# Layer 0's mixture of experts: token rows by indirect DMA and transposes instead of one-hot products, and the overflow block in line as a 33rd expert

## The chip, the core and the metric

The kernel runs on one core of one Trainium2 chip. The metric is the device time of one execution in microseconds. The engines are TensorE (PE in the profile; its weight loads are PEld), VectorE (DVE), ScalarE (ACT), GpSimd (POOL) and SyncE (SP). All weights come from HBM through DMAs that SP issues; POOL issues a few DMAs of its own. Each engine works through its own queue in order.

## The reference

A trunk of two layers over 256 latent tokens (`x`) and 256 context tokens (`ctx`) of width 1024. Each layer is a mixer (layer 0: neighbourhood attention and a state-space branch; layer 1: two kinds of attention), a layer norm, and a mixture of 32 experts with two experts per token, chosen within one of four groups. Layer 0 sends all 512 tokens through its experts, layer 1 only the 256 latent ones. What the change touches:

```python
def hier_moe(h, wg, bg, we, be, w1, w3, w2):
    ...
    gate = g_gate * jax.nn.softmax(e_top, axis=-1)
    expert = g_sel * MOE_EXPERTS_PER_GROUP + e_idx
    return grouped_expert_mlp(h, expert, gate, w1, w3, w2)

def expert_block(args):          # inside grouped_expert_mlp
    xi, e = args                 # the rows of the tokens that chose expert e
    return (jax.nn.silu(xi @ w1[e]) * (xi @ w3[e])) @ w2[e]
...
out = jnp.zeros((t_tok + 1, dm), h.dtype).at[slot_tok].add(yb * slot_w[:, None])
```

An expert's weights are two matrices of 1024x512 and one of 512x1024, 6.29 MB in float32.

## The kernel before

`moe` handles one layer's experts. Every expert has 64 slots (`CAP`); `dest` holds for each token its two slot numbers, and tokens that find no slot among the 64 go to overflow blocks of 64 slots (`odest`), of which the first is nearly always used and further ones run in a loop on a count found at run time. Tokens lie in tiles of 128: four in layer 0 (`nt == 4`), two in layer 1.

Experts are gathered in groups of four (256 slots). `onehots` writes a 0/1 matrix of tokens by slots, and `gather` multiplies the token rows with it, so that the result is the group's rows, transposed, in `xg`. The rows are kept as a high and a low part (`h2h`, `h2l`), and a gather has four steps (`jp`), each of 4 tiles x 2 parts x 2 = 16 products of 128x256 into the PSUM tile `pg`. `gather_ahead` does the first three tiles of group 0 before the last tile is there. `group_gates` gets the gate of each slot by a product of the one-hot matrix with `gdr` (`pgs`, then `gs`), in two halves of 128 slots.

The loop in `moe` is a software pipeline over the experts. In turn e it issues the first half of the up-projection of expert e (`expert_up`, PSUM tile `a`), two combine steps, a gather step, the transposes of the expert before (`hp`), the second half of the up-projection, two more combine steps, and the down-projection of the expert before (`py`). A combine step (`combine_steps`) multiplies a pair of experts' outputs (`yh`, `yl`) with the turned one-hot matrix (`poT`, `ohT`) into `pcm`; VectorE multiplies it with a row of the modulation (`ym`), and POOL or VectorE adds it to the residual `S`. `pg` and `pcm` share a pair of PSUM buffers. Matrix products are kept in program order (`mmp`, `trp`); what else runs is ordered by a scheduler.

Weights go through a ring of twelve 1 MB buffers, eight called `ringw` and four called `raw` (`whalf`), so loads run up to two experts ahead. SP issues them in order, each when its buffer is free.

After the loop comes `overflow`: if there is a first block, `block` loads one expert's weights by a number read from `ov`, and computes it, start to end, on rows that were gathered during the last experts (`block_first`); then further blocks follow in a second loop. Behind it the layer norm scales the four tiles of `S`, and `mixer1` begins with transposes of `S` (`xT`) and products with weights that `unit` loads and splits (`w1h`, `w1l`).

Of the kernel before, what the change touches and what calls it, by code (L numbers as in the profile page):

```python
# [27 lines left out]
I32 = mybir.dt.int32  # L28
# [39 lines left out]
class Trunk:  # L68
# [68 lines left out]
    def run(self):  # L137
# [9 lines left out]
        self.mods = self.dram.tile([2, 2, 6144], F32, name="mods")  # L147
        self.prow = self.dram.tile([2, 2, 2, DM], F32, name="prow")
# [30 lines left out]
    def late_consts(self):  # L179
        nc, I = self.nc, self.I  # L180
        nc.gpsimd.dma_start(self.iota, self.bcast(I['iota'], 256))
        nc.gpsimd.dma_start(self.istack, I['istack'])
        nc.gpsimd.memset(self.one2, 1.0)
# [219 lines left out]
    def moe_tiles(self, nt):  # L403
        mp = self.moep
        self.h2h = mp.tile([128, nt, 8, 128], F32R, name="h2h")
        self.h2l = mp.tile([128, nt, 8, 128], F32R, name="h2l")
# [447 lines left out]
    def enter_moe(self, pool, layer, i, t, rows, R, nt):  # L854
# [126 lines left out]
    def moe(self, layer, tiles):  # L981
# [4 lines left out]
        with ExitStack() as es:  # L986
            with self.pool("exp", "right") as ep:
# [9 lines left out]
                def group(q):  # L997
                    ohs[q] = self.onehots(ep, nt, self.dest, 256.0 * q, 256) if q else self.oh0
                    X[q], st = self.gather(ep, nt, ohs[q], 256, None if q else self.pg0)
                    steps.extend(st)  # L1000

                def gates(q):
                    gs[q] = self.group_gates(ep, nt, ohs[q], 4 * q)
# [25 lines left out]


                for e in range(33):
                    cur = cur if e == 0 else begin(e) if e < 32 else None
                    if e % 2 == 0 and e < 32:
# [4 lines left out]
                    fill(2 if e > 28 else 1, steps)  # L1038
# [7 lines left out]
                    if e % 4 == 2 and e < 28:  # L1046
# [4 lines left out]
                    if prev:  # L1051
                        k = (e - 1) % 2
                        c = C[(e - 1) // 2]
                        if k == 0:
                            self.combine_turn(ep, nt, c)
                        self.expert_down(prev, c, k)
                        if k:
                            todo += self.combine_steps(ep, tiles, c)
                    if e == 0:
                        group(1)  # L1060
                        fill(2, steps)
# [33 lines left out]
    def group_gates(self, ep, nt, oh, e):  # L1095

        gs = ep.tile([64, 4], F32, name="gs", bufs=2)
        for i in range(2):
            pg = self.ps([128, 2, 32], "pgs")
            for t in range(nt):  # L1100
                self.mmp(pg.rearrange("p a b -> p (a b)"), oh[:, t, 128 * i:128 * i + 128], self.gdr[:, t], start=(t == 0), stop=(t == nt - 1))
# [758 lines left out]
```

## Time and profile before

| | us |
|---|---|
| median of 3 runs | 1883.29 |
| lowest and highest | 1879.22, 1886.46 |
| profiled execution | 1881.46 |
| its span, first to last instruction | 1879.6 |

| busy in the span | us | share |
|---|---|---|
| TensorE (products) | 1721.9 | 92% |
| VectorE | 975.9 | 52% |
| ScalarE | 507.7 | 27% |
| GpSimd | 358.3 | 19% |

Layer 0's experts take roughly 570 to 1130 us of the span, the first overflow block up to 1158, and layer 1's experts the last 480 us. Products are pipelined: a product's duration in a row is longer than the distance to the next one, so the distance between two starts is what a series of products costs. A row of the order of time shows the start, the time to the end of the last of the merged instructions, the engine, the line and operation, what it writes and reads, how many instructions were merged, and in brackets how long the engine stood idle before and what released it.

### The profile page before, as it was taken

What the parts mean: (1) busy time and instruction counts of PE and PEld (TensorE: products, weight loads), DVE (VectorE), ACT (ScalarE), POOL (GpSimd) and SP (SyncE); (2) the same over time, 40 slices, a digit from 0 to 9 for tenths busy, and PEclk for the clock granted to TensorE, in tenths of its full rate; (3) what the DMA queues carried; (4) which work ended last, traced back from release to release, by engine and by line L of the source; (5) the groups of instructions that cost most, each with busy time, mean ns of one, the idle gap of its engine ahead of it and who ended that gap; (6) DMA issues with size and microseconds to landing.
All of it is one profiled execution on the core that took longest, in us unless ns stands there. A gap on an engine that the chain in (4) does not pass through costs nothing. (4 is left out here: it accounts for less than half of the span.)

```text
span 1879.6 us, 22554 instructions
## 1 busy us (share of the span) xinstructions
PE 1721.9 (92%) x8481; PEld 915.1 (49%) x8481; DVE 975.9 (52%) x2007; ACT 507.7 (27%) x986; POOL 358.3 (19%) x297
## 2 busy tenths in 40 slices
PE   6999989988999999999999984889979999999995
PEld 3665656666555444444444441766444444444442
DVE  2454579896664453444443455774463433333335
ACT  2423344443212111111111111457431112111111
POOL 2212124443104111111111112422030100100101
PEclk9999999999999999999999986889989999999997
DMA  9655366645437999999999941345249999999993
GB/s 330 222 188 180 102 207 206 219 153 160 188 124 302 419 370 362 368 372 368 380 359 361 378 176 58 106 150 191 112 164 419 420 419 419 419 420 420 419 420 154
DMA packets 100371, 526.52 MB, mean 280 GB/s; under 512 B 20320, under 2 KB 24416, under 8 KB 46624
## 3 DMA queue, kind: packets, MB, share of 16 engines
q1 hardware_dynamic: 97456, 517.59, 71.5%
q0 software_dynamic: 2800, 7.42, 1.2%
q8 instruction: 70, 1.15, 0.2%
q14 instruction: 45, 0.37, 0.1%
HBM read 523.76 MB, written 1.20 MB: 279 GB/s over the span
## 5 line engine op out<-in xcount | busy, mean ns | idle before, releaser
L193 PE MATMUL a<-ringw,xg 128*64 128x512 f32 x1584 | 366.0, 601 | 0.8 <-DVE xg L1642 0.8
L193 PEld LDWEIGHTS a<-ringw,xg 128*64 128x64 f32 x1584 | 112.5, 138 | 208.7 <-issue 197.2
L1123 DVE TENSOR_TENSOR ym<-pcm,mod 128x512 f32<-128x512 f32 x136 | 90.6, 687 | 186.5 <-PE pcm L193 185.5
L1694 DVE TENSOR_TENSOR yl<-py,yh 64x512 fp32r<-64x512 f32 x130 | 89.4, 688 | 184.0 <-ACT yh L1693 183.9
L1124 POOL TENSOR_TENSOR S<-S,ym 128x512 f32<-128x512 f32 x68 | 87.1, 1281 | 466.8 <-DVE ym L1123 466.8
L1693 ACT ACTIVATE yh<-py 64x512 fp32r<-64x512 f32 x130 | 76.8, 591 | 297.3 <-PE py L193 247.8
L193 PE MATMUL py<-ringw,g 128*64 128x512 f32 x640 | 151.9, 617 | 0.5 <-ACT g L1677 0.5
L1124 POOL TENSOR_TENSOR S<-S,two 128x512 f32<-128x512 f32 x32 | 40.9, 1277 | 411.6 <-DVE two L1123 411.6
L193 PE MATMUL a<-raw,xg 128*64 128x512 f32 x496 | 116.0, 606 | 1.8 <-DMA raw<-in_moe_w_dram 1.8
L105 PE MATMUL pfm<-hTh,wh 128*128 128x512 f32 x256 | 105.8, 415 | 8.2 <-ACT up L639 5.5
L193 PE MATMUL pg<-two,h2h 128*128 128x256 f32 x408 | 90.6, 304 | 18.4 <-DVE ym L1123 10.4
L212 PE MATMUL adaps<-adw,cs 128*32 128x512 f32 x384 | 96.6, 645 | 11.5 <-DMA adw<-in_ada_w_dram 11.4
L100 POOL TENSOR_TENSOR wl<-raw,wh 128x512 fp32r<-128x512 f32 (+1 forms) x46 | 59.8, 1306 | 231.1 <-ACT wh L99 173.9
L106 PE MATMUL pfm<-hTh,wl 128*128 128x512 f32 x256 | 103.1, 403 | 0.0
L107 PE MATMUL pfm<-hTl,wh 128*128 128x512 f32 x256 | 101.0, 401 | 0.0
L1668 ACT ACTIVATE sa<-a 64x512 f32<-64x512 f32 x65 | 38.4, 591 | 222.3 <-PE a L193 222.3
L193 PE MATMUL pcm<-yh,ohT 128*128 128x512 f32 (+1 forms) x200 | 91.9, 460 | 6.8 <-DVE ym L1123 4.0
L1123 DVE TENSOR_TENSOR two<-pcm,S 128x512 f32<-128x512 f32 x64 | 42.7, 688 | 95.6 <-PE pcm L193 95.1
L193 PE MATMUL py<-raw,g 128*64 128x512 f32 x400 | 91.4, 598 | 0.5 <-ACT g L1677 0.5
L193 PEld LDWEIGHTS pg<-two,h2h 128*128 128x128 f32 x408 | 64.8, 196 | 49.3 <-DVE ym L1123 21.7
L193 PE MATMUL pg<-two,h2l 128*128 128x256 f32 x408 | 84.0, 288 | 2.0 <-DVE h2l L49 2.0
L193 PEld LDWEIGHTS py<-ringw,g 128*64 128x64 f32 x640 | 45.0, 141 | 83.6 <-issue 77.9
(510 smaller groups left out, 2931.9 us busy)
## 6 DMA issues: line engine op xcount, KB each, us to landing
ringw<-in_moe_w_dram SPq DMA_DIRECT2D x278, 1024.0 KB, 10.3
raw<-in_moe_w_dram SPq DMA_DIRECT2D x112, 1024.0 KB, 8.3
adw<-in_ada_w_dram SPq DMA_DIRECT2D x96, 512.0 KB, 5.4
raw<-in_w_in_dram SPq DMA_DIRECT2D x18, 1024.0 KB, 7.2
bc<-atd SPq DMA_DIRECT2D x16, 512.0 KB, 6.7
raw<-in_w_out_dram SPq DMA_DIRECT2D x4, 1024.0 KB, 5.1
raw<-in_o_w_out_dram SPq DMA_DIRECT2D x4, 1024.0 KB, 5.1
bias<-in_rpb_dram SPq DMA_DIRECT2D x8, 256.0 KB, 4.5
```

The costliest lines, as they stand in the source:

```text
L100: (eng or nc.vector).tensor_tensor(lo, src, hi, OP.subtract)
L105: mm(out, ah, bh, start=start, stop=False)
L106: mm(out, al, bh, start=False, stop=False)
L107: mm(out, ah, bl, start=False, stop=stop)
L193: return self.tc.keep_in_program_order(self.nc.tensor.matmul(*args, **kw))
L212: self.nc.tensor.matmul(p[32 * g:32 * g + 32, :], self.cs[:, j, :], w[:, (g - g0) * 512:(g - g0 + 1) * 512], start=(j == 0), stop=(j == 7))
L1123: nc.vector.tensor_tensor(m, p, self.rows5[t // 2][:, k], OP.mult)
L1124: (nc.gpsimd if i % 2 == 0 else nc.vector).tensor_tensor(S[:, t, k], S[:, t, k], m, OP.add)
L1668: self.nc.scalar.activation(s, a[0:64, :], AF.Silu)
L1693: nc.scalar.activation(c[h][0][r], py[q], AF.Copy)
L1694: V.tensor_tensor(c[h][1][r], py[q], c[h][0][r], OP.subtract)
```

## The change

In layer 0, each token tile's `h2` is stored by SP to an array in HBM, `h2d`. The number of each token stands as a 33rd column beside the gates in `gdr`, so that the product that yields the gates of a slot yields the number of its token too. VectorE copies that number to an integer tile `ix`, and POOL issues an indirect DMA that brings the 128 rows of 4 KB of half a group into `rows`, a tile that takes the memory of `h2l`. `turn_rows` transposes them into `pg`: a step is four transposes instead of 16 products. Group 0 and all of layer 1 gather as before. The gates of a group are made ahead of its rows, in the first expert of the group before; two turn steps stand in the second expert, one each in the third and fourth.

The first overflow block becomes expert 32 of the loop, always computed, with its weights' place read by SP; its one-hot matrix is made in expert 28's turn, its rows are fetched and its gates computed in expert 29's, and its steps stand in those of 30 and 31. Only further blocks are left behind the loop. Ahead of those SP issues the first loads of layer 1 (`ahead1`), and two tiles of `S` are scaled by VectorE and two by ScalarE, not three and one.

```diff
@@ enter_moe
+        if nt == 4:
+            nc.sync.dma_start(self.h2d[128 * i:128 * i + 128, :], h2)
@@ moe
+                    if q == 0 or nt == 2:
+                        X[q], st = self.gather(ep, nt, ohs[q], 256, None if q else self.pg0)
+                        steps.extend(st)
+                    else:
+                        if q == 1:
+                            self.rows_begin()
+                        rows = self.next_rows()
+                        X[q], st = self.turn_rows(ep, rows, 256)
+                        steps.extend([lambda: gates(q, rows)] + st)
...
                 def begin(e):
+                    if e == 32:
+                        at = nc.values_load(self.ov[0:1, 0:1], engines=[mybir.EngineType.SP], min_val=0, max_val=31)
+                        return self.expert_begin(ep, layer, None, B['xg'][:, :, 0, :], lambda: B['gs'], load=self.expert_at(layer, at))
...
+                nb = 33 if nt == 4 else 32
+                for e in range(nb + 1):
+                    cur = cur if e == 0 else begin(e) if e < nb else None
+                    if e == 32 and cur:
+                        C[16] = B['c']
...
-                    fill(2 if e > 28 else 1, steps)
+                    fill(2 if e > 28 or nt == 4 and e % 4 == 1 else 1, steps)
...
-                    if e % 4 == 2 and e < 28:
+                    if e % 4 == 2 and e < 28 and nt == 2:
                         gates(e // 4 + 1)
...
+                if layer == 0:
+                    self.ahead1 = {n: self.unit_raw(n, 256) for n in ('o_gkv', 'o_gq0')}
+                    self.rings, self.ring_k = self.rings[:1], 0
                 self.overflow(ep, layer, tiles, B)
...
-                    if t != 2:
+                    if t % 2 == 0:
                         V.tensor_scalar(S[:, t], S[:, t], r, m, op0=OP.mult, op1=OP.add)
@@ new functions
+    def fetch(self, ep, row, p):
+        n = p.shape[0]
+        ix = ep.tile([128, 1], I32, name="ix", bufs=4)[:n]
+        self.nc.vector.tensor_copy(ix, p)
+        self.nc.gpsimd.indirect_dma_start(row, None, self.h2d[:, :], bass.IndirectOffsetOnAxis(ap=ix, axis=0))
...
+    def turn_rows(self, ep, rows, n):
...
+        def step(jp):
+            p = self.ps([128, 2, 256], "pg")
+            for i in range(2):
+                for a in range(0, n, 128):
+                    m = min(128, n - a)
+                    self.trp(p[:, i, a:a + m], rows[:m, a // 128, 2 * jp + i::8])
...
@@ group_gates
+            if rows is not None:
+                self.fetch(ep, rows[:, i], pg[:, 0, 32:33])
@@ route_rest
+        self.gdr = self.ep.tile([128, nt, 2, 33], F32R, name="gdr")
...
+        V.tensor_copy(self.gdr[:, :, 0, 32], self.tok[:, 0:nt])
+        V.tensor_copy(self.gdr[:, :, 1, 32], self.tok[:, 0:nt])
@@ block_first
+            if nt == 4:
+                B['oh'] = self.onehots(ep, nt, self.odest, float(NSLOT), CAP)
+                return
...
+        def rows():
+            B['xg'], B['steps'] = self.turn_rows(ep, self.block_rows(ep, nt, B['oh']), CAP)
...
+        return B, [begin, rows, rest] + turn if nt == 4 else [begin] + turn + [rest]
@@ overflow
+        if nt == 4:
+            return more()
```

How the queues change at the places that the prediction speaks of. On TensorE, part of a turn of the loop in the middle of a group before (`a` are up-projections, `py` down-projections):

```order
L193 MATMUL a_5009<-ringw,xg 64x512 x8
L193 MATMUL pcm<-yh,ohT 128x512
L193 MATMUL pcm<-yl,ohT 128x512
L193 MATMUL pcm<-yh,ohT 128x512
L193 MATMUL pcm<-yl,ohT 128x512
L193 MATMUL pg<-two_4794,h2h 128x256 x2
L193 MATMUL pg<-two_4794,h2l 128x256 x2
```

and at the same place after:

```order
L197 MATMUL a_5056<-ringw,xg 64x512 x8
L197 MATMUL pcm<-yh,ohT 128x512
L197 MATMUL pcm<-yl,ohT 128x512
L197 MATMUL pcm<-yh,ohT 128x512
L197 MATMUL pcm<-yl,ohT 128x512
L201 MATMUL pg<-ident,rows 128x128 x4
L201 MATMUL hp<-ident,sa 128x64 x4
```

The pair of `h2h` and `h2l` rows stands four times in a row before; four transposes take the place of those eight rows.

On POOL, at the start of the expert stage, before:

```order
L1022 DMA yh<-in_ln_g_dram 128x512
L1022 DMA yl<-in_ln_b_dram 128x512
L1025 TENSOR_TENSOR S<-S,yh 128x512 x6
L1025 TENSOR_TENSOR S<-S,yl 128x512
L1025 TENSOR_TENSOR S<-S,yh 128x512 x2
L1025 TENSOR_TENSOR S<-S,yl 128x512 x7
```

and after:

```order
L1043 TENSOR_TENSOR S<-S,yh 128x512 x4
L1126 DMA rows<-h2d,ix 128x1024
L1043 TENSOR_TENSOR S<-S,yh 128x512 x2
L1043 TENSOR_TENSOR S<-S,yl 128x512
L1043 TENSOR_TENSOR S<-S,yh 128x512 x2
L1126 DMA rows<-h2d,ix 128x1024
L1043 TENSOR_TENSOR S<-S,yl 128x512 x7
```

The two fetches of the first group's rows stand among the sixteen operations that scale and shift `S`, behind the fourth and the ninth.

On VectorE, at the entry of layer 1, after (the statistics, the two splits, the reciprocal root, of which the first rows stand here, and the scaled tiles):

```order
L841 BN_STATS lnst<-S 128x6 x8
L842 BN_AGGR lnmv<-lnst 128x2 x2
L100 TENSOR_TENSOR w1l<-raw,w1h 128x512
L842 BN_AGGR lnmv<-lnst 128x2
L100 TENSOR_TENSOR w1l<-raw,w1h 128x512
L842 BN_AGGR lnmv<-lnst 128x2
L844 TENSOR_SCALAR lnn<-lnmv 128x4
```

Before, the four BN_AGGR stand together, the two splits come behind the root, one of them ahead of the three tiles of `S` and one behind them; now the splits are among the statistics and two tiles of `S` follow the root.

## Rows read from the trace of the kernel before

**Rows 1.** The page, busy time: engine, us, share of the span, instructions.

```profile
PE 1721.9 (92%) x8481; PEld 915.1 (49%) x8481; DVE 975.9 (52%) x2007; ACT 507.7 (27%) x986; POOL 358.3 (19%) x297
```

**Rows 2.** Stretches: length; PE, PEld, DVE, ACT, POOL busy (instructions); clock, DMA share, GB/s.

```profile
611.00:658.00 47.00, 45.72 (x222) 20.61 (x222) 22.13 (x39) 7.88 (x15) 6.42 (x5) 1.00 1.01 418
...
768.00:836.00 68.00, 64.26 (x322) 30.58 (x320) 31.25 (x52) 11.01 (x20) 10.26 (x8) 1.00 0.95 370
...
1400.00:1800.00 400.00, 390.51 (x1863) 164.86 (x1860) 143.49 (x241) 76.92 (x144) 43.08 (x34) 1.00 1.01 418
```

**Rows 3.** TensorE's waits, 577 to 1092 us: us in total, times, longest.

```profile
PE pgs L193 <- DVE gs L1103: 12.5, 8, 1.9
```

**Rows 4.** Order of time, TensorE, in layer 0's experts.

```profile
615.65 3.60 PE L193 MATMUL a<-ringw,xg 128*64 128x512 f32 x16
...
804.88 0.50 PE L193 MATMUL pg<-two,h2h 128*128 128x256 f32 x2 [0.39 <-DVE ym L1123]
...
806.98 0.69 PE L197 MATMUL hp<-ident,sa 64*128 64x64 f32 x4
807.60 3.65 PE L193 MATMUL a<-ringw,xg 128*64 128x512 f32 x16
...
1091.64 3.60 PE L193 MATMUL a<-ringw,xg 128*64 128x512 f32 x16
```

**Rows 5.** Order of time, TensorE, at the entry of layer 1.

```profile
1185.27 0.62 PE L189 MATMUL xT<-ident,S 128*128 128x128 f32 x4
1185.65 0.48 PE L321 MATMUL pgk<-w1h,h1Tl 128*128 128x256 f32 x2
```

**Rows 6.** SP's order of time, then two POOL transfers: KB each, us to landing.

```profile
547.59 2.04 SPq L426 DMA_DIRECT2D raw<-in_moe_w_dram  x2
551.02 2.04 SPq L426 DMA_DIRECT2D ringw<-in_moe_w_dram  x2
...
mod<-mods POOLq DMA_DIRECT2D x1, 512.0 KB, 8.9
...
mod<-mods POOLq DMA_DIRECT2D x1, 512.0 KB, 3.9
```

**Rows 7.** Order of time at the start of the expert stage, TensorE and POOL.

```profile
586.68 3.65 PE L193 MATMUL a<-ringw,xg 128*64 128x512 f32 x16
...
600.65 3.60 PE L193 MATMUL a<-ringw,xg 128*64 128x512 f32 x16
...
583.79 7.50 POOL L1025 TENSOR_TENSOR S<-S,yh 128x512 f32<-128x512 f32 x6 [11.94 <-ACT yh L1023]
```

**Rows 8.** Order of time around the last experts and the block.

```profile
1096.30 0.39 PE L193 MATMUL pgs<-one,ovg 128*64 128x2 f32 x4
...
1101.02 1.06 PE L197 MATMUL poT<-ident,two 128*64 128x128 f32 x4 [0.24 <-DVE ovgs L1711]
...
1111.26 0.69 DVE L1124 TENSOR_TENSOR S<-S,ym 128x512 f32<-128x512 f32 x1
...
1130.47 7.09 PE L193 MATMUL a<-ringw,xg 128*64 128x512 f32 x32
...
1146.29 0.50 PE L193 MATMUL pcm<-yh,ohT 64*128 64x512 f32 x1 [0.69 <-ACT yh L1693]
...
1156.17 1.26 POOL L1124 TENSOR_TENSOR S<-S,ym 128x512 f32<-128x512 f32 x1 [1.23 <-DVE ym L1123]
...
1156.72 1.25 DVE L1124 TENSOR_TENSOR S<-S,ym 128x512 f32<-128x512 f32 x1
```

**Rows 9.** Order of time at the entry of layer 1, VectorE and TensorE.

```profile
1160.81 4.84 DVE L837 BATCH_NORM_STATS2 lnst<-S 128x6 f32<-128x512 f32 x8 [2.83 <-issue]
...
1172.91 1.77 DVE L100 TENSOR_TENSOR w1l<-raw,w1h 128x512 fp32r<-128x512 f32 x1 [4.49 <-ACT w1h L99]
...
1174.61 5.10 DVE L1076 TENSOR_SCALAR S<-S,rsq_y,lnm 128x1024 f32<-128x1024 f32 x3
...
1183.11 0.56 PE L319 MATMUL pgk<-w1h,h1Th 128*128 128x256 f32 x1
```

More of the change, by code (lines that the diff above doesn't have):

```diff
@@ L147, in run @@
         self.mods = self.dram.tile([2, 2, 6144], F32, name="mods")
+        self.h2d = self.dram.tile([512, DM], F32, name="h2d")
         self.prow = self.dram.tile([2, 2, 2, DM], F32, name="prow")
@@ L1028, in moe @@
                 prev = None
-                for e in range(33):
-                    cur = cur if e == 0 else begin(e) if e < 32 else None
-                    if e % 2 == 0 and e < 32:
+                nb = 33 if nt == 4 else 32
[3 more added lines that the diff above has]
+                        C[16] = B['c']
+                    elif e % 2 == 0 and e < 32:
                         C[e // 2] = dict(oh=ohs[e // 4], sl=slice(64 * (e % 4), 64 * (e % 4) + 128))
@@ new lines, in next_rows @@
+    def next_rows(self):
+        self.rows_n = 1 - self.rows_n
+        return self.rows[:, self.rows_n]
+    def turn_rows(self, ep, rows, n):
+        nc, V = self.nc, self.nc.vector
+        k = n // 64
+        xg = ep.tile([128, 8, 4, 64], F32, name="xg", bufs=2)
+        def step(jp):
[4 more added lines that the diff above has]
+                    self.trp(p[:, i, a:a + m], rows[:m, a // 128, 2 * jp + i::8])
+            o = xg[:, 2 * jp:2 * jp + 2, 0:k, :]
+            src = p[:, :, :n].rearrange("p i (e s) -> p i e s", s=64)
+            if jp % 2:
+                nc.scalar.activation(o, src, AF.Copy)
+            else:
+                V.tensor_copy(o, src)
+        return xg, [lambda jp=jp: step(jp) for jp in range(4)]
@@ L1098, in group_gates, with block_rows @@
+    def block_rows(self, ep, nt, oh):
+        p = self.ps([CAP, 2], "pgs")
+        for t in range(nt):
+            self.mmp(p, oh[:, t, :CAP], self.gdr[:, t, 0, 31:33], start=(t == 0), stop=(t == nt - 1))
+        rows = self.next_rows()
+        self.fetch(ep, rows[:CAP, 0], p[:, 1:2])
+        return rows
+    def group_gates(self, ep, nt, oh, e, rows=None):
+        gs = ep.tile([64, 4], F32, name="gs", bufs=3)
         for i in range(2):
-            pg = self.ps([128, 2, 32], "pgs")
+            pg = self.ps([128, 2, 33], "pgs")
@@ L1126, in combine_steps, with unit_raw @@
         return [lambda i=i, t=t, h=h: step(i, t, h) for h in range(2) for i, t in enumerate(tiles)]
+    def unit_raw(self, name, w):
+        return [self.load([128, 4, w], self.I[name][:, 4 * i:4 * i + 4]) for i in range(2)]
     def mixer1(self):
@@ L1204, in unit @@
             def unit(name, w, eng=V):
-                raws = [self.load([128, 4, w], I[name][:, 4 * i:4 * i + 4]) for i in range(2)]
+                raws = self.ahead1.pop(name, None) or self.unit_raw(name, w)
                 hi = pp.tile([128, 8, w], F32R, name="w1h", bufs=2)
@@ L1725, in rest, with expert_at @@
             self.combine_turn(ep, nt, B['c'], CAP)
-        return B, [begin] + [lambda j=j: B['steps'][j]() for j in range(4)] + [rest]
+        turn = [lambda j=j: B['steps'][j]() for j in range(4)]
+        return B, [begin, rows, rest] + turn if nt == 4 else [begin] + turn + [rest]
+    def expert_at(self, layer, e):
+        return lambda nm: self.I[nm][layer, ds(e, 1)].rearrange("a b c -> (a b) c")
     def block(self, ep, layer, tiles, e, xg, c):
-        load = lambda nm: self.I[nm][layer, ds(e, 1)].rearrange("a b c -> (a b) c")
-        E = self.expert_begin(ep, layer, None, xg, c['gs'], load=load)
+        E = self.expert_begin(ep, layer, None, xg, c['gs'], load=self.expert_at(layer, e))
         for k in range(2):
@@ L1752, in more @@
                 oh = self.onehots(ep, nt, self.odest, base, CAP)
-                xg, steps = self.gather(ep, nt, oh, CAP)
+                xg, steps = self.turn_rows(ep, self.block_rows(ep, nt, oh), CAP) if nt == 4 else self.gather(ep, nt, oh, CAP)
                 for step in steps:
```

34 lines of the change are left out of this document (16 added, 18 removed).

## The prediction, written before the changed kernel ran

> **What bounds the kernel now.** I read the page first: TensorE is busy 92% of the span [rows 1]. A share of the whole span says nothing on one stage, so the table by stretches came next [rows 2]. The change lives in layer 0's experts, about 577 to 1130 us. There TensorE is busy 64.3 of 68 us while the loads run at 370 GB/s; in the expert stage of layer 1 (1400 to 1800 us) they run at 418 GB/s, and so they did for a while at the start of layer 0's stage. So 418 is what the loads can do, and in layer 0 they have some 12% in hand: TensorE sets the pace there, not the weights. The third view, TensorE's order of time, shows the period: the first up-projection of expert 3 starts at 615.65, that of expert 31 at 1091.64 [rows 4]: 476.0 us for 28 experts, 17.0 each, 68.0 a group of four. What TensorE waits for in that stretch is little: the second half of the gate products waits for VectorE, 12.5 us in 8 times [rows 3], and the one-hot gather waits 0.39 us for a PSUM buffer [rows 4]. Shortening TensorE's own work in the loop therefore shortens the stage, until the loads end last.
>
> **The loop.** A gather step (16 products of 128x256) runs from 804.88 to 806.98, where the transposes of hp start: 2.10 us [rows 4]. The new step is four 128x128 transposes of a tile read with stride 8. The trace of before has that very form at the entry of layer 1: four issued at 1185.27, the next instruction at 1185.65 [rows 5], 0.38 us, and with 0.1 us to the next 0.48. Each step saves 1.62 us. Between those two up-projections lie 28 steps (six groups and the block), so 45.4 us. Against it: in every fourth expert two turns now stand together, and the second takes the PSUM buffer that the last combine product has only just filled. It waits for one more VectorE product, about the 0.39 us of the gather's wait plus one 0.69 us operation [rows 4, 8], 1.1 us, seven times: 7.5 us. The block's gates, which stood behind expert 31's first up-projection, move to expert 29 and so into this stretch: from 1096.30 to 1101.02, 4.7 us [rows 8]. The gates of a group move from the third expert to the first of the group ahead, and cost what they cost now (the same wait for VectorE). Their 66th column and two small index copies are taken at nothing, under the wait of [rows 3]; without it they are some 0.3 us a group. Sum: 476.0 - 45.4 + 7.5 + 4.7 = 442.8 us.
>
> Does the other limit allow it? 28 experts read 28 x 6.29 MB = 176.1 MB; the rows add 6 x 1.05 MB and the block's 0.26, together 182.7 MB, which at 418 GB/s [rows 2] is 437 us. That is 6 us under TensorE's 442.8: the two limits now nearly meet, where before they were 12% apart. Two queues that are both almost full do not run at the larger of the two, so I allow 3 us: **gain 30**. The ends: 36 (loads at the best rate, second turns free), and 15 (each row read costs twice its bytes, 453 us, and another 1 us in each of eight fetches).
>
> **The start of the stage.** Here the change adds a wait. Expert 1 wants the first two turns right after its first up-projection, and their rows must have been fetched. In POOL's queue, the second piece of order above, the first fetch stands behind four of the multiplications of S, the second behind five more. That train starts at 583.79 and each takes 1.25 us [rows 7], so the first fetch is issued at 588.8. How long POOL needs for an indirect fetch no row shows; I take the length of its neighbour, 1.25 us, where a plain one takes less. The second is then issued at 588.8 + 1.25 + 6.25 + 1.25 = 597.6. Landing: a POOL transfer of the same 512 KB took 3.9 us with the queues empty and 8.9 us when at least four loads of 1 MB had been issued in the 6.2 us before it [rows 6]; in the middle, 604. TensorE is ready for the turns at about 589 (up-projection of expert 1 now from 586.68 [rows 7], about a microsecond earlier without the products before it). So it stands still for about 15 us. Then the two turns, hp, the second up-projection, poT and the down-projection take about 9.3 us, and expert 2 begins at 613.3 instead of 600.65 [rows 7]. Expert 2 itself is 3.3 us shorter (no gather step, no gates). **Loss about 10**, ends 4 and 18. Behind the fetches nothing urgent is queued: seven multiplications of S, wanted only by the first combine products, in expert 3. The four stores of h2 on SP's queue wait for VectorE and hold back the loads behind them; what the last one holds are loads for expert 1's down-projection and expert 2. I cost them at nothing; were those weights late, the wait for the rows covers them.
>
> **The fetches in the loop** are issued in the first expert of a group and wanted in the next. Between stand hp 0.62 us [rows 4], an up-projection of 3.6, combine products 1.0, a down-projection 3.5, an up-projection and again combine products: 13.2 us, less the copy and the issue about 11. Both landings in [rows 6] are under that, so I take no stall.
>
> The Trainium skill, page "DMA: Bandwidth & Descriptors", section "SWDGE vs HWDGE vs iDMA", says that POOL's queue and SP's feed different internal queues of a DMA engine and that the engine takes them in turn. [...]
>
> **The tail.** From expert 31's first up-projection (1091.64) to the last addition of the block (1156.72 + 1.25 = 1157.97) are 66.3 us [rows 4, 8]: the block begins at 1130.47 only when everything before it is through, and its own chain of 27.5 us has no company. In line it runs as expert 32. From the same point: the rest of expert 31 at the loop's pace 14.6 us, expert 32 and expert 31's down-projection 13.3, four combine products, hp and expert 32's down-projection 6.8, its evacuation 1.4, and then twelve combine steps, of which VectorE does one in about 1.3 us (eight of them from 1146.29 to 1157.97 [rows 8]): 15. Sum 51.1. **Gain 15**, ends 10 (weights of expert 32 land last) and 18.
>
> **The entry of layer 1.** Before: statistics begin at 1160.81; VectorE then waits 4.49 us for a weight split whose load was issued only after the loop, does it, and scales three tiles, until 1179.71 [rows 9], 18.9 us; TensorE starts 3.4 us later at 1183.11. After: two splits of 0.7 us stand among the statistics, their weights loaded ahead; statistics to about 9.0 us, then two tiles of 1.7 each: 12.4. **Gain 6**, ends 3 and 8 (ScalarE has eight splits ahead of its two tiles).
>
> **Sum.** 30 + 15 + 6 - 10 = 41 us. The profiled execution took 1881.46 us (span 1879.6), so 1840.5; the median of the runs is 1.8 us longer: **1842 us**.
>
> **Rivals.**
> - *The rows land late* (the slower side). Place: the two turns in the second expert of each group. If fetches take L us under full loads, each of the other seven pairs costs L - 11. Nothing is lost up to 11; 1.5 us over that is 1852; the sign turns to slower than 0.5% (above 1892.7) from L = 11 + 51/7 = 18.3, and L = 20 gives 1842 + 63 = 1905. Against: 8.9 us [rows 6]. For: no row shows an indirect fetch, and here two stand in the queue. There is a second way to late rows: VectorE's addition of S takes 0.69 us alone (1111.26) and 1.25 when POOL's runs (1156.72 beside 1156.17) [rows 8], so the two engines hold each other up, and VectorE could hold up POOL's fetch. By these rows that is about 1 us a fetch, inside the 11. The Trainium skill, page "SBUF — State Buffer", section "SBUF: two separate sides", gives a reason: POOL cannot write its descriptors while VectorE holds the pair of ports they share. The trace agrees on the sharing; what it does to an indirect fetch no run shows. Chance 0.06.
> - *The loads become the bound.* Row reads cost more than their bytes; the loop gains 15 to 23: 1849 to 1857. For: only 6 us lie between the limits. Chance 0.2.
> - *The change does not do what it says in the loop*: the steps saved were hidden and the loop gains nothing: 1842 + 30 = 1872. Against: 370 GB/s against 418. Chance 0.07.
> - *The start costs little* (rows land at once, POOL's train is short) and the limits do not disturb each other: 1842 - 6 - 6 = 1830. Chance 0.12.
> - The forecast, 1835 to 1849: chance 0.55.
>
> **How the numbers follow.** The range takes in the forecast, the cheap start and the load-bound case with its ends: 1825 to 1868; outside lie late rows and most of the 1872 case. A measurement of this kernel can tell about 0.5%, 9.4 us. Faster by more than that (under 1873.9): forecast, start, load bound and half of the third rival, less some overlap of bad ends, 0.87. Within 0.5%: 0.08. Slower: 0.05.
>
> **What would show it.** In the profile of the changed kernel: a group of four experts in about 63 us with loads near 415 GB/s; one idle stretch of TensorE of about 15 us near 589 that ends with a DMA of rows; no wait for rows at the later turns (a wait there is the first rival, waits for ringw or raw the second); from expert 31's first up-projection to the last addition about 51 us; statistics to the last scaled tile 12 to 13 us. If the group's period is still 68, the first step is wrong; if the start shows no idle stretch, the fifth.

## The result, and the profile after

Median **1830.77 us** (1823.99 to 1835.46) against 1881.26 us (1878.47 to 1886.46) for the kernel before in the same comparison: ratio **0.972** (95% interval 0.9682 to 0.9757). A second comparison over more rounds gave 1829.12 us and 0.9706 (0.9679 to 0.9733). The forecast was 1842 us, 11 us too slow, inside its range, but outside the forecast's own band of 1835 to 1849; the kernel is faster, as forecast. The profiled execution of after took 1835.46 us (span 1833.7).

The page of after, busy time by engine, the answer to [rows 1]:

```profile
PE 1680.1 (92%) x8093; PEld 871.2 (48%) x8093; DVE 968.9 (53%) x2025; ACT 507.8 (28%) x987; POOL 374.6 (20%) x313
```

The table of stretches, the answer to [rows 2]: the loop from expert 3 to expert 31, then layer 1's experts (last columns: granted clock, DMA share, GB/s):

```profile
633.00:1067.00 434.00, 417.50 (x1914) 175.99 (x1912) 217.53 (x374) 77.40 (x141) 85.51 (x69) 0.98 1.01 420
1400.00:1780.00 380.00, 370.09 (x1772) 158.03 (x1769) 141.05 (x231) 70.96 (x134) 33.75 (x27) 1.00 1.01 421
```

TensorE's busy share is the same 92%, and says as little as before. The second view tells more: in layer 0's loop the loads now run at 420 GB/s, as fast as in layer 1, where before they ran at 370. What TensorE waits for from 560 to 1067 us (total, times, longest; the three largest of nine), the answer to [rows 3]:

```profile
PE pg L201 <- DMA rows<-h2d,ix: 10.7, 2, 8.0
PE pgs L197 <- DVE gs L1176: 8.1, 9, 1.0
PE pg L201 <- DVE ym L1196: 7.9, 21, 0.4
```

The rows are waited for twice, both times at the start of the stage; nowhere later does TensorE wait for rows, and never for ringw or raw. In the loop, TensorE's order of time answers [rows 4]: a turning step, the two steps that stand together in every fourth expert, and a group's gates:

```profile
632.79 3.60 PE L197 MATMUL a<-ringw,xg 128*64 128x512 f32 x16
...
637.84 0.71 PE L201 MATMUL pg<-ident,rows 128*128 128x128 f32 x4 [0.32 <-DVE ym L1196]
638.48 0.69 PE L201 MATMUL hp<-ident,sa 64*128 64x64 f32 x4
...
652.31 0.53 PE L197 MATMUL pgs<-gdr,two 128*128 128x66 f32 x4
653.85 0.60 PE L197 MATMUL pgs<-gdr,two 128*128 128x66 f32 x4 [1.01 <-DVE gs L1176]
654.38 0.69 PE L201 MATMUL hp<-ident,sa 64*128 64x64 f32 x4
655.00 5.35 PE L197 MATMUL a<-ringw,xg 128*64 128x512 f32 x16
...
670.02 1.30 PE L201 MATMUL pg<-ident,rows 128*128 128x128 f32 x8 [0.39 <-DVE ym L1196]
671.25 0.69 PE L201 MATMUL hp<-ident,sa 64*128 64x64 f32 x4
...
1066.80 3.60 PE L197 MATMUL a<-ringw,xg 128*64 128x512 f32 x16
```

A step takes 0.64 us (637.84 to 638.48) where the one-hot step took 2.10, and from expert 3 (632.79) to expert 31 (1066.80) are 434.0 us instead of 476.0.

All profiled executions can be laid side by side by five marks, each read off the order of time as in the rows here: the first product of the one-hot gather (end of layer 0's mixer), the first up-projections of experts 3 and 31, the end of the last addition to S, and the first product of layer 1's keys (pgk). The columns are the distances between them (us); the experiments are told below.

| kernel | mixer 0 to | to expert 3 | loop, to expert 31 | tail, to last addition | entry, to pgk | rest | span |
|---|---|---|---|---|---|---|---|
| before | 552.2 | 63.5 | 476.0 | 66.3 | 25.1 | 696.5 | 1879.6 |
| before, again (8) | 551.9 | 61.9 | 477.9 | 65.7 | 25.7 | 698.5 | 1881.5 |
| after | 561.0 | 71.8 | 434.0 | 54.1 | 19.0 | 693.9 | 1833.7 |
| after, again (12) | 556.7 | 71.1 | 431.6 | 57.0 | 19.0 | 694.0 | 1829.3 |
| 1 S scaled later | 559.2 | 63.5 | 433.2 | 54.1 | 19.0 | 694.1 | 1823.0 |
| 2 group 1 one-hot | 556.9 | 61.3 | 430.9 | 54.1 | 18.9 | 691.4 | 1813.5 |
| 3 turns twice | 560.6 | 71.7 | 444.9 | 54.3 | 19.0 | 694.4 | 1845.0 |
| 4 fewer weights | 555.3 | 70.9 | 431.6 | 57.0 | 19.0 | 691.7 | 1825.4 |
| 5 block behind | 559.3 | 70.9 | 431.4 | 60.0 | 20.4 | 694.5 | 1836.4 |
| 6 no loads ahead | 559.7 | 72.4 | 434.3 | 54.1 | 22.3 | 697.4 | 1840.1 |
| 7 old scaling | 563.0 | 70.8 | 431.5 | 54.1 | 19.0 | 693.8 | 1832.2 |
| 9 before, one load more | 556.3 | 61.9 | 477.6 | 66.0 | 25.3 | 693.1 | 1880.1 |
| 10 that load on SP | 552.1 | 74.1 | 434.5 | 54.1 | 18.9 | 693.9 | 1827.5 |
| 11 both, 2 and 10 | 552.9 | 61.3 | 430.5 | 57.0 | 18.9 | 694.2 | 1814.7 |

So the change gains 42 us in the loop, 12 in the tail, 6 in the entry and 3 in the rest, and gives back 8 at the start of the expert stage and 9, which nothing in the prediction stood for, in the mixer ahead of it.

### The profile page after: what moved, and what is told of

Same layout as the page of the kernel before. It is cut to its first block, busy times and chain, and to the rows that moved or that the text cites. A ratio compares the mean times of both kernels' runs of the same rounds, so it can differ in the third digit from the quotient of the medians.

```text
span 1833.7 us, 21779 instructions
## 1 busy us (share of the span) xinstructions
PE 1680.1 (92%) x8093; PEld 871.2 (48%) x8093; DVE 968.9 (53%) x2025; ACT 507.8 (28%) x987; POOL 374.6 (20%) x313
## 5 line engine op out<-in xcount | busy, mean ns | idle before, releaser
L197 PE MATMUL a<-ringw,xg 128*64 128x512 f32 x1584 | 371.4, 611 | 0.8 <-DVE ovbase L1833 0.5
L197 PE MATMUL py<-ringw,g 128*64 128x512 f32 x640 | 146.0, 597 | 0.0
L216 PE MATMUL adaps<-adw,cs 128*32 128x512 f32 x384 | 97.6, 656 | 13.5 <-DMA adw<-in_ada_w_dram 13.4
L197 PEld LDWEIGHTS py<-ringw,g 128*64 128x64 f32 x640 | 43.8, 136 | 81.1 <-issue 74.1
L197 PE MATMUL pcm<-yl,ohT 128*128 128x512 f32 (+1 forms) x200 | 81.1, 406 | 0.6 <-DVE yl L1773 0.6
L197 PEld LDWEIGHTS pcm<-yh,ohT 128*128 128x128 f32 (+1 forms) x200 | 38.2, 191 | 91.4 <-issue 64.8
L1748 DVE SCALAR_TENSOR_TENSOR sa<-sa,gs,a 64x512 f32<-64x512 f32 x64 | 47.9, 749 | 52.0 <-ACT sa L1747 50.6
```

Source lines behind the costliest of these rows:

```text
L197: return self.tc.keep_in_program_order(self.nc.tensor.matmul(*args, **kw))
L216: self.nc.tensor.matmul(p[32 * g:32 * g + 32, :], self.cs[:, j, :], w[:, (g - g0) * 512:(g - g0 + 1) * 512], start=(j == 0), stop=(j == 7))
L1748: self.nc.vector.scalar_tensor_tensor(s, s, E['gs'], a[64:128, :], op0=OP.mult, op1=OP.mult)
```

## Experiments

### What sets the loop: TensorE or the loads

Two limits nearly meet there (layer 1's loads run at 421 GB/s, so 420 is taken as their ceiling). Experiment 3 adds work to TensorE (each transpose of a turning step twice), experiment 4 takes work from the loads (w2_halves is 1 in layer 0 and 2 in layer 1).

```diff
-            for i in range(2):
+            for i in (0, 1) * 2:
```

> Every turning step of layer 0 makes its transposes twice into the same place, which changes no result; the 25 to 28 steps in the loop cost 0.64 us of TensorE each in after. Theory (TensorE sets the loop, the loads keep up at 420 GB/s by their lead of 12 buffers): the loop from expert 3 to expert 31 grows from 434 to about 450 us and the time to about 1848 us (1843 to 1852). Rival (the loads set the loop, 26.2 MB per group at 420 GB/s is 62.4 us where a group takes 61 to 62): the added work fits into waits, the loop stays at 434 to 437 and the time at 1831 to 1835.

```diff
-        r = [self.whalf(src[:, a * h:a * h + a]) for h in range(2)]
+        r = [self.whalf(src[:, a * h:a * h + a]) for h in range(self.w2_halves)] * 2
```

> In layer 0 the second half of each expert's third matrix isn't loaded; the first half is used in its place. A group of four experts then loads 22.0 MB instead of 26.2, which at 420 GB/s takes 52.4 us, and all of TensorE's work is kept. Theory (TensorE sets the loop): expert 3 to expert 31 takes 425 to 434 us as in after (434), at most the 5 us slower up products after the gates being saved, and the time stays at 1824 to 1831 us apart from small changes at the start. Rival (the loads set the loop): the distance falls towards 7 x 52.4 = 367 us, at least below 415, and the time below 1810.

Measured: e3 1845.01 us (1839.94 to 1848.46), loop 444.9 us; e4 1828.06 us (1823.9 to 1834.0), loop 431.6 us. The stretch of the loop in e4, from the table of stretches:

```profile
626.00:1058.00 432.00, 415.53 (x1916) 175.93 (x1914) 217.43 (x374) 77.54 (x142) 85.59 (x69) 0.98 0.94 358
```

A doubled step in e3, TensorE's order of time:

```profile
637.41 1.16 PE L201 MATMUL pg<-ident,rows 128*128 128x128 f32 x8 [0.32 <-DVE ym L1196]
638.51 0.69 PE L201 MATMUL hp<-ident,sa 64*128 64x64 f32 x4
```

With the loads at 358 GB/s instead of 420 the loop is as long as in the second profile of after (431.6 us). With four transposes more in a step, which cost 1.10 - 0.64 = 0.46 us, the loop grows by 11 to 13 us. Between its two marks stand 25 full steps and two half ones (the block's 64 rows); 25 of 0.46 are 11.5, and summed over the trace, from start to start, all of them take 27.2 us in e3 and 16.7 in after. The expectation had taken 0.64 for the added transposes, which is the length of a whole step, and was too high by that. TensorE sets the loop, and the loads at their ceiling cost nothing.

### The start: what the rows wait for

In after, the lists of rows, the fetches and the turns stand so in order of time:

```profile
591.61 0.16 DVE L1125 CAST ix<-pgs 128x1 int32<-128x1 f32 x1 [0.54 <-PE pgs L197]
...
593.22 0.16 DVE L1125 CAST ix<-pgs 128x1 int32<-128x1 f32 x1 [1.22 <-PE pgs L197]
...
596.03 1.05 POOL L1126 DMA_INDIRECT rows<-h2d,ix  x1 [0.16 <-issue]
597.10 2.50 POOL L1043 TENSOR_TENSOR S<-S,yh 128x512 f32<-128x512 f32 x2
...
601.67 0.38 PE L201 MATMUL pg<-ident,rows 128*128 128x128 f32 x1 [2.76 <-DMA rows<-h2d,ix]
603.41 1.01 POOL L1126 DMA_INDIRECT rows<-h2d,ix  x1 [0.16 <-issue]
...
610.00 1.76 PE L201 MATMUL pg<-ident,rows 128*128 128x128 f32 x7 [7.95 <-DMA rows<-h2d,ix]
```

The second list is ready at 593.38, its fetch goes out 10 us later, and the turn starts 6.6 us after that. Experiment 1 lets POOL's multiplications of S wait for the list (the factor that they need is worked out from it), so that both fetches go first; experiment 2 gathers this one group by one-hot products as before. In e1 the lines that scale S are a function, scale_S, called behind group 1's gates:

```diff
-                alpha = ep.tile([128, 1], F32, name="alpha")
-                V.tensor_scalar(alpha, self.odest[:, nt - 1, 1:2], 0.0, ALPHA, op0=OP.mult, op1=OP.add)
...
+                    alpha = ep.tile([128, 1], F32, name="alpha")
+                    V.tensor_scalar(alpha, self.ix if nt == 4 else self.odest[:, nt - 1, 1:2], 0.0, ALPHA, op0=OP.mult, op1=OP.add)
...
                         fill(2 if nt == 2 else 1, steps)
+                        if nt == 4:
+                            scale_S()
...
```

> The 16 multiplications of S on POOL (1.26 us each) are made to wait for the second list of rows of group 1, so that both of that group's fetches are issued ahead of them. In the trace of after the lists were ready at 591.77 and 593.38 us, the fetches were issued at 596.03 and 603.41, behind 4 and 7 of these multiplications, and TensorE then waited 2.8 and 8.0 us for the rows. Theory (the start's loss is POOL's queue): the fetches go at about 591.8 and 593.4, the rows are there 5.6 to 6.6 us later at about 600, the two waits shrink from 10.7 to 1 to 2 us, the distance from the first gather product to expert 3's first up product falls from 71.75 to 62 to 63 us, and the time from 1831 to about 1822 us (1818 to 1826). Rival (the landing of the rows themselves is what is slow, behind the expert loads): the landing grows as the issue comes earlier, the distance stays above 68, the time at 1828 or more. Rival (the later multiplications of S hold up the additions of the first combine): the first addition on POOL, 637.9 in after with 25 us of idle time ahead of it, comes later; not expected, the multiplications would end at about 615.

In e2:

```diff
-                    if q == 0 or nt == 2:
+                    if q <= 1 or nt == 2:
...
-                        if q == 1:
+                        if q == 2:
                             self.rows_begin()
...
-                    if e % 4 == 2 and e < 28 and nt == 2:
+                    if e % 4 == 2 and e < 28 and (nt == 2 or e == 2):
                         gates(e // 4 + 1)
...
-                        fill(2 if nt == 2 else 1, steps)
+                        fill(2, steps)
```

> Group 1 (experts 4 to 7) is gathered by one-hot products as in before, groups 2 to 7 and the block as in after. Theory: the start is that of before (first gather product to expert 3's first up product 63.5 us, where after has 71.75), and the loop from there to expert 31 keeps its 434 us, as group 1's gather lies ahead of it in both: about 1831 - 8 = 1823 us (1818 to 1828). The rows' wait of 10.7 us is gone from TensorE's waits. Rival (group 1's 4 one-hot steps, 1.62 us each dearer than the turned ones, cost as much as the wait): 1829 to 1833.

Measured: e1 1822.65 us (ratio 0.9664, 0.9648 to 0.9679), 63.5 us to expert 3; e2 1816.98 us (0.9643, 0.9625 to 0.9662), 61.3 us to expert 3, a little faster than its expectation had room for. (In after the second fetch stood behind nine multiplications, not the seven of e1's expectation.) In e1 the same instructions stand so:

```profile
592.20 1.05 POOL L1132 DMA_INDIRECT rows<-h2d,ix  x1 [11.61 <-DVE gs L1182]
...
593.80 0.98 POOL L1132 DMA_INDIRECT rows<-h2d,ix  x1 [0.55 <-DVE gs L1182]
...
594.81 8.61 POOL L1044 TENSOR_TENSOR S<-S,yh 128x512 f32<-128x512 f32 x7
...
600.70 0.38 PE L201 MATMUL pg<-ident,rows 128*128 128x128 f32 x1 [1.96 <-DMA rows<-h2d,ix]
601.74 1.05 PE L201 MATMUL pg<-ident,rows 128*128 128x128 f32 x7 [0.67 <-DMA rows<-h2d,ix]
```

The wait falls from 10.7 to 2.6 us. From issue to turn it is now longer (592.20 to 600.70 and 593.80 to 601.74, 8.5 and 7.9 us, where it was 5.6 and 6.6). The first fetch gained nothing by that: counted from the end of the mixer it was issued 2.0 us earlier and took 2.9 longer. The second was issued 7.8 us earlier and took 1.4 longer: the loss was POOL's queue ahead of it, not the transfer. Experiment 2 is still 2 us shorter in this stretch, although it does the one-hot products. The table of stretches shows a difference that fits: in after TensorE's granted clock falls here, in e2 it doesn't. After, from 590 to 600 and from 606 to 618 us:

```profile
590.00:594.00 4.00, 2.84 (x10) 2.10 (x12) 1.79 (x14) 2.56 (x4) 3.07 (x3) 0.58 1.01 428
594.00:600.00 6.00, 4.91 (x16) 1.25 (x12) 0.00 (x0) 0.00 (x0) 5.82 (x6) 0.71 0.97 397
...
606.00:612.00 6.00, 2.00 (x10) 1.68 (x10) 0.69 (x1) 0.21 (x1) 6.00 (x6) 0.50 0.37 139
612.00:618.00 6.00, 6.00 (x26) 2.19 (x26) 0.23 (x1) 1.63 (x4) 1.02 (x1) 0.79 0.00 0
```

The same stretches in e2:

```profile
590.00:594.00 4.00, 4.00 (x24) 1.77 (x19) 0.00 (x0) 0.07 (x1) 4.00 (x4) 1.00 1.01 422
594.00:600.00 6.00, 6.00 (x42) 4.31 (x42) 0.69 (x1) 0.98 (x2) 6.00 (x6) 1.00 1.01 423
...
606.00:612.00 6.00, 6.00 (x30) 2.19 (x28) 1.38 (x2) 1.04 (x3) 0.62 (x1) 1.00 1.02 431
```

In after, group 1's gates, which wait for VectorE, stand alone ahead of expert 1's first up-projection; TensorE has gaps there, and the clock stands at the lower level (0.50 is 1.2 GHz) for part of the next products. In e2 one-hot products stand at this place, and it stays at 1.00. In e1 it falls as in after (0.66 from 590 to 600 us), and that up-projection takes 5.48 us where one at the full clock takes 3.65:

```profile
593.26 5.48 PE L197 MATMUL a<-ringw,xg 128*64 128x512 f32 x16
```

So the one-hot products, which are dearer than the turns but need no rows, cost less than the gap. (That the clock and the 2.6 us of waits left in e1 make up its distance to e2 is read from the rows, not tested apart.)

### The tail: in line, or cheaper work

Experiment 5 puts the block behind the loop again:

```diff
-                nb = 33 if nt == 4 else 32
+                nb = 32
...
-        if nt == 4:
-            return more()
         n0 = nc.values_load(ov[0:1, NOV:NOV + 1], min_val=0, max_val=1)
...
+            if nt == 2:
+                more()
+        if nt == 4:
             more()
```

> As after, but the block beyond 64 slots stands behind the loop again as in before, in a loop of its own that is run once; its rows are still fetched and turned. Theory (the order is what gains, not the gather): the distance from expert 31's first up product to the last addition to S, 66.3 us in before and 54.1 in after, goes back to 63 to 67 us, as the block's up, gate, turn and down products stand in a chain again, and the time rises by 9 to 13 us to 1840 to 1844 us. Rival (the block's cheaper gather brings the gain of the tail): the distance stays at 54 to 58 and the time at 1831 to 1835.

Measured: 1838.46 us (0.9729, 0.9708 to 0.975), tail 60.0 us: between the two expectations. So of the 12.2 us that the tail gained, 6.3 are there without the block in line. They are hardly a saving of the whole: the block's gates, which took 4.7 us of TensorE's time behind expert 31's first up-projection [rows 8], now stand ahead of it, inside the loop, and cost 5.5 us there. (In before, the up-projection behind them also ran slower. Its row in before, then the same one in e5:)

```profile
1102.68 5.58 PE L193 MATMUL a<-raw,xg 128*64 128x512 f32 x16
...
1068.07 3.65 PE L197 MATMUL a<-raw,xg 128*64 128x512 f32 x16
```

The block in line is worth the other 5.9 in the tail (3.0 against the second profile of after, with its tail of 57.0) and 1.4 in the entry. In the whole time e5 lies 7.7 and 9.3 us above the two medians of after, but by the ratios, each against before in its own comparison, only 2 to 4 us, and the intervals overlap; so the gain in the tail is shown, and its size in the whole is not. (What the 6.3 us consist of is read from the rows, not tested apart.)

### The entry of layer 1: loads ahead, or the scaling

Experiment 6 takes back the loads ahead, experiment 7 the division of the scaling.

```diff
-                    self.ahead1 = {n: self.unit_raw(n, 256) for n in ('o_gkv', 'o_gq0')}
-                    self.rings, self.ring_k = self.rings[:1], 0
+                    self.ahead1 = {}
```

> As after, but the first four weight tiles of layer 1 are no longer loaded ahead at the end of the loop; the scaling of S is as in after (two halves on DVE, two on ACT). Theory (loading ahead carries nearly all of the entry's gain): the distance from the last addition to S to the first key product of layer 1, 25.1 us in before and 19.0 in after, goes back to 23 to 26 us, and the time rises by 4 to 7 us to 1835 to 1838 us. Rival (the scaling carries it): 19 to 21 us and 1831 to 1833.

```diff
-                    if t % 2 == 0:
+                    if t != 2:
```

> As after, but three of the four scalings of S stand on DVE and one on ACT, as in before. Theory (with the first tiles split early, POOL is done with them when the scalings run, and three on DVE take 2.3 us at the 0.77 us each of after, where before's took 5.1): the distance from the last addition to the first key product stays at 19 to 20 us, the time at 1830 to 1833 us. Rival (the scaling carries the gain): 21 to 25 us and 1833 to 1837.

Measured: e6 1841.34 us (0.9751, 0.9735 to 0.9767), entry 22.3 us; e7 1832.4 us (0.9697, 0.968 to 0.9714), entry 19.0 us. The entry in after, the answer to [rows 9]:

```profile
1123.06 4.85 DVE L841 BATCH_NORM_STATS2 lnst<-S 128x6 f32<-128x512 f32 x8 [2.17 <-issue]
...
1134.08 1.53 DVE L1102 TENSOR_SCALAR S<-S,rsq_y,lnm 128x1024 f32<-128x1024 f32 x2
1134.08 2.37 ACT L1104 ACTIVATE S<-S,lnm,rsq_y 128x1024 f32<-128x1024 f32 x2 [7.04 <-DVE lnm L847]
...
1139.85 0.56 PE L323 MATMUL pgk<-w1h,h1Th 128*128 128x256 f32 x1
```

The scaling in e6, and POOL's splits beside it:

```profile
1132.14 8.75 POOL L100 TENSOR_TENSOR w1l<-raw,w1h 128x512 fp32r<-128x512 f32 x6 [12.23 <-ACT w1h L99]
...
1136.33 3.43 DVE L1101 TENSOR_SCALAR S<-S,rsq_y,lnm 128x1024 f32<-128x1024 f32 x2
```

Two scalings take 1.53 us on VectorE when POOL's splits are done, and 3.43 us beside them. With the loads ahead, POOL is done in time and the division of the scaling is worth nothing (e7, as expected). Without them the entry is 3.3 us longer than in after, a little less than expected and still 2.9 shorter than in before; and the rest of layer 1 is 3.5 us longer too, perhaps because the splits that follow come later; that was not tested. Together these are 6.8 us. In the whole, e6 is 11 to 12 us above the medians of after, but before, too, was slower in its comparison (1887.68 us), and by the ratios the distance is 6 to 8 us. The 4 to 7 expected counted up to the first product of the keys only.

### The 9 us in the mixer

No line of layer 0's mixer is in the diff, but its end came 8.9 us later in the profile. The added load of the token numbers (one small issue on POOL) makes the scheduler order the mixer's instructions otherwise, on all engines, from 327 to 472 us above all. Experiment 8 is the kernel before once more, 9 adds that load alone to it, 10 moves it in after to SP at the head of the expert code, which restores the old order of the mixer. Experiment 11 joins 2 and 10, and 12 is after once more. The edit of e9:

```diff
         nc.gpsimd.dma_start(self.istack, I['istack'])
+        self.tok = self.cons.tile([128, 4], F32, name="tok")
+        nc.gpsimd.dma_start(self.tok, bass.AP(tensor=I['num'].tensor, offset=I['num'].offset, ap=[[1, 128], [128, 4]]))
...
```

The edit of e10, against after:

```diff
-        nc.gpsimd.dma_start(self.tok, bass.AP(tensor=I['num'].tensor, offset=I['num'].offset, ap=[[1, 128], [128, 4]]))
...
                 self.ep = ep
+                if nt == 4:
+                    num = I['num']
+                    nc.sync.dma_start(self.tok, bass.AP(tensor=num.tensor, offset=num.offset, ap=[[1, 128], [128, 4]]))
```

> The kernel before, unchanged, once more with a profile: how far does the first layer's mixer vary from run to run? Its end, the first gather product, stood at 552.2 us in the profiled run of before and at 561.0 in that of after; in the four experiments, whose mixer is after's in its source, at 559.2, 556.9, 560.6 and 555.3. If the 8.9 us are the run's and not the change's, this one lies anywhere between 552 and 561; if the changed order of instructions costs them, at 551 to 553.

> The kernel before with one thing added: the load of the token numbers (2 KB, one issue on POOL's queue among the first layer's constants), which nothing reads. The program's order in the first layer's mixer then is, instruction for instruction, that of after, since the scheduler that orders the work reacts to the issue; all else is as in before. The first gather product stood at 552.2 and 551.9 us in two profiled runs of before, and at 555.3 to 563.0 (mean 559.4) in eight of after and its variants. Theory (the new order of the mixer costs the 7 us, in its stretch from 327 to 472 us): first gather product at 556 to 563, the time 4 to 10 us above before's in the same call. Rival (the 7 us come with something else of the change): 551 to 553, the time within 2 us of before's.

> As after, but the token numbers are loaded by SP at the head of the expert layer's code instead of by POOL in the mixer; the mixer's order is again that of before. Theory (the order costs 7 us): first gather product at 551 to 553 us, all else as in after, the time 5 to 9 us below after's 1831, about 1824 us. Rival: 555 to 563, 1829 to 1833 us.

> Both at once: group 1 by one-hot products as in the second experiment and the token numbers loaded by SP. Theory (the two losses are independent): 1817 - 7 = 1810 us (1806 to 1813), first gather product at 551 to 553, from there to expert 3's first up product 61 us, to expert 31's another 431. Rival (the mixer's time isn't the order's): 1815 to 1819.

> The kernel after, unchanged, over more rounds and with a second profile, to be held against the tenth experiment, which differs from it by the mixer's order alone (0.9677 of before, 0.9658 to 0.9696). In the profiles the mixer ends at 551.9 to 552.9 us with the old order (4 profiles) and at 555.3 to 563.0 with the new one (9), yet the ninth experiment, before with the new order, took no longer than before (1.0002, 0.9986 to 1.0017). Theory (the order costs time here): ratio 0.971 to 0.973, 5 to 10 us above the tenth. Rival (what the mixer loses is given back later or varies from run to run): 0.967 to 0.969. First gather product at 556 to 563 either way.

The first gather product, one row of TensorE's order of time each, for three of the profiles. In before:

```profile
552.15 0.80 PE L193 MATMUL pgb<-two,h2h 128*128 128x256 f32 x2
```

In 9, before with the new order:

```profile
556.33 0.80 PE L196 MATMUL pgb<-two,h2h 128*128 128x256 f32 x2
```

In after:

```profile
561.04 0.80 PE L197 MATMUL pgb<-two,h2h 128*128 128x256 f32 x2
```

Four profiles with the old order end at 551.9 to 552.9 us, ten with the new one at 555.3 to 563.0 (mean 558.8); the two of after alone are 4.4 us apart. That the added load, and with it the order, moves the mixer's end is shown. What it costs in the whole is not: e9 took 1885.75 us against 1885.47 (1.0002, 0.9986 to 1.0017), no loss at all, with a rest of layer 1 shorter by 3 to 5 us than in the two profiles of before; e10 took 1824.92 us (0.9677, 0.9658 to 0.9696), and after again 0.9706 (0.9679 to 0.9733), some 5 us apart with intervals that overlap. And in e10, part of the mixer's gain is lost again ahead of expert 3 (74.1 us instead of 71 to 72). Why e9 loses nothing stays open.

Experiment 11 is the fastest kernel of all: **1813.76 us** (0.9624, 0.9607 to 0.9641), 3 us below experiment 2, where 7 were expected.

## Why the prediction was right, and where it was off

The mechanism held: TensorE set the loop's pace, the loads had the room, the gather step shrank, and what was lost lay behind POOL's queue at the start. That the number came so near is in part luck, since errors cancelled. The profile of after is 45.9 us shorter than that of before, where the sum had 41: the loop gained 12 us more than forecast, the start lost 1.7 less and the rest of layer 1 gave 2.6, but the mixer lost 8.9 and the tail fell 2.8 short. The other 6 of the 11 us are that the profiled execution of after was 4.7 us slower than its median, and that 1.8 us had been added for the median. The time met the 1830 of the rival "the start costs little" (0.12) for another cause: the start did cost 8 us, and only the rival's second half, that the limits do not disturb each other, held.

- **The loop** (forecast gain 30, ends 15 and 36; measured 42; a group took 60.7 or 62.2 us for the 63 forecast). The turned step was priced too low, 0.48 us for 0.64, and counted too often: 28 times, where after has 25 full steps and two half ones between the marks. Summed over the trace from start to start, the one-hot steps took 58.5 us in before and the turned ones 16.7 in after, 41.9 less instead of 45.4. Three terms against it did not come. The second of two turns was to wait 1.1 us, seven times; the row at 670.02 shows both in one piece, with one wait of 0.39 us, the same as for one turn. The 3 us for two limits that nearly meet, which stood on no row, were not needed (e4). And a group's gates, taken as unchanged, take 2.07 us at their new place (652.31 to 654.38) where they took 2.92 in before:

```profile
812.21 0.53 PE L193 MATMUL pgs<-gdr,two 128*128 128x64 f32 x4
814.59 0.60 PE L193 MATMUL pgs<-gdr,two 128*128 128x64 f32 x4 [1.85 <-DVE gs L1103]
815.13 3.65 PE L193 MATMUL py<-ringw,g 128*64 128x512 f32 x16
```

  That saved 5.9 us over the loop. The block's gates cost 5.5 us in the loop (4.7 forecast). No term stood for the clock: the up-projections, some of which now follow gates at the lower clock, take 7.2 us more in the loop than in before, and the down-projections, which followed the gates there, 4.0 less. The upper end, 36, seems to be what loads of 437 us leave (39) less the 3 us, and was too low by those.
- **The loads as the bound** (rival, 0.2): fell. The arithmetic was good (434.0 us at 420 GB/s are 182.3 MB, 182.7 were forecast), but a limit that is just met showed no price here.
- **The start** (forecast loss 10, ends 4 and 18; measured 8.3 against the profile of before and 9.9 against its second one). Right in place and cause, with 10.7 us of waits in two pieces where one of 15 was forecast. The fetches were issued at 596.03 and 603.41, 7.4 us apart, as the forecast's 1.25 + 6.25 has it (its 597.6 holds the second issue too); an indirect issue takes 1.0 us here, not 1.25. Not foreseen: the fall of the clock.
- **Late rows in the loop** (rival, 0.06): fell; no wait for rows behind the start. It was nearer than the forecast says: a landing took up to 12.4 us, where 11 were reckoned with, and from the second fetch of a group to its turn there were 12.5 to 14.2 us.
- **Nothing gained in the loop** (rival, 0.07): fell, by the 42 us.
- **The tail** (forecast 51.1 us, gain 15; measured 54.1, gain 12). The largest part of the difference lies between the end of expert 31's down-projection and that of expert 32's, 8.5 us where 6.8 were forecast. TensorE waits there for expert 31's outputs, which ScalarE and VectorE copy, and for a PSUM buffer that VectorE empties:

```profile
1096.32 0.50 PE L197 MATMUL pcm<-yh,ohT 128*128 128x512 f32 x1 [0.69 <-ACT yh L1772]
1097.04 0.50 PE L197 MATMUL pcm<-yl,ohT 128*128 128x512 f32 x1 [0.22 <-DVE yl L1773]
...
1099.84 0.50 PE L197 MATMUL pcm<-yh,ohT 128*128 128x512 f32 x1 [0.56 <-DVE ym L1196]
...
1100.51 3.65 PE L197 MATMUL py<-ringw,g 128*64 128x512 f32 x16
```

  My reason for the gain was half right: e5 shows that 6.3 us do not come from the block's place, and the rows put most of them on its gates, which moved into the loop and are paid for there.
- **The entry** (forecast gain 6; measured 6.2; statistics to last scaled tile, ScalarE's, 13.4 us for 12.4: 11.0 up to the scaling and 2.4 for it, where 9.0 and 3.4 were forecast). Right, though by the loads ahead alone.
- **Not in the sum**: the mixer's new order (8.9 us in the profile, 0 to 6 in the time), and the rest of layer 1, 2.6 us shorter, which no run explains.

## What to carry to other kernels

Price a change by what stands on the bounding engine, and look at the first use of a new transfer apart from the steady state: its list, its issue queue and its landing lie bare there, and keeping the old way for the first group alone was worth 12 us here. A gap on TensorE costs more than its length when the granted clock falls behind it. Where a scheduler orders the code, compare the order of stages that the diff does not touch, and ask for an effect in the whole time before believing one in a stage.

## What the runs showed of the hardware

- **Clock.** Products after a short gap ran at the lower level for a while. In after a wait of 1.01 us stands in a group's gates, and the granted clock was 0.72 from 655 to 661 us behind it: the up-projection there took 5.35 us instead of 3.65 (row 655.00). It fell so in about every second group, and groups took 62.2 or 60.7 us by that alone; why only in some is open. In the tail, whether it falls ahead of expert 32's down-projection went with the tail's 57.0 or 54.1 us in the four profiles read for it (after, 2, 11, 12); in the second profile of after it did:

```profile
1093.57 6.07 PE L197 MATMUL py<-ringw,g 128*64 128x512 f32 x16
```

- **Indirect fetches.** 128 rows of 4 KB take POOL 0.94 to 1.24 us to issue. From issue to landing the 15 fetches of after (one of them of 64 rows) took a median of 9.5 us, in the loop with the loads at 420 GB/s:

```profile
rows<-h2d,ix POOLq DMA_INDIRECT x15, 9.5
```

  Whether a POOL transfer passes the loads issued before it is open: the one of 8.9 us in [rows 6] landed at about 563 us, when those loads, too, were through (401 to 418 GB/s from 554 to 560 us, 12 from 562 to 563).
- **VectorE and POOL.** A scaling of S takes 0.77 us alone and 1.72 beside POOL's splits. By the Trainium skill, page "SBUF — State Buffer", section "SBUF: two separate sides", POOL cannot write a DMA's descriptors while VectorE runs an operation that holds the pair of ports they share. The trace of after shows no such cost in the issues: none took over 1.24 us, with VectorE busy for half of the loop. Whether it is a part of the landings no run shows.
